# Linear attention of a hybrid layer taken four blocks at a time, with a new table of delays

## The chip, the cores and the metric

The kernel runs on one core of a Trainium2 chip. The metric is the device time of one execution in microseconds (us), as the median of three runs. Smaller is better. All arithmetic is float32; where the kernel uses the replicated form of it, `fp32r`, a float32 number is split into a high and a low part, and three products (high by high, low by high, high by low) take the place of one.

## The reference

One layer of a hybrid decoder with 1024 positions and 1024 channels. The normalised input goes through one wide projection, whose columns feed three groups: gated linear attention (GLA, 4 heads, key width 64, value width 128), an S5 state-space group with a Gelu and a gate, and an RG-LRU recurrent group. Their outputs go through one output projection, and a gated MLP with a short convolution follows. The part that the change touches is the GLA, which works on chunks of 64 positions:

```python
bc = jnp.cumsum(chunks(gk, DK), axis=3)              # log decay within a chunk
scores = einsum('bhncd,bhnsd->bhncs', qc * exp(bc - b_mid), kc * exp(b_mid - bc))
scores = jnp.where(causal, scores, 0.0)
o_intra = einsum('bhncs,bhnsv->bhncv', scores, vc)
kv = einsum('bhnsd,bhnsv->bhndv', kc * exp(b_last - bc), vc)
def step(S, inp):                                    # over the chunks
    dec, kv_n = inp
    return dec[..., None] * S + kv_n, S
o_inter = einsum('bhncd,bhndv->bhncv', qc * exp(bc), S_prev)
o = rmsnorm(o_intra + o_inter, norm_g) * silu(g)
```

## The kernel before

*How the order of the work comes about.* The program is written out once, on the host, in a single order. A small planner decides it: each piece of side work is a generator (`gla_task`, `gla_out`, the S5 and RG-LRU tasks, the gate `s5_glu`, `t_pre`), and each of its yields puts it back in a heap with a due time. `run(filler)` takes the task whose due time has come by a model clock `clk`, and otherwise lets the filler write one more piece of the big matrix products. Only matrix products move `clk` on. How long a task rests behind its yield is in the table `DLY`, under the task's name and the number of the yield. `ORDER` lists the column tiles of the wide projection in the order in which the filler comes to them. Every engine then works strictly in the order that was written, so DLY and ORDER set what stands behind what on each engine, in the queue of SyncE (SP), which issues the DMAs, too.

*The GLA.* Its heads come in two pairs (`p` = 0, 1: tasks gla0 and gla1), the 1024 positions in two halves (`hf`) of four blocks of 128 positions, that is of two chunks. `gla_prep` makes the decayed queries and keys of a half on VectorE (DVE) and ScalarE (ACT). TensorE (PE) transposes the keys (`psk2`; ACT copies them to `km`). Then the half goes in two steps `j` of two blocks each. A step writes the scores (`psc`) and their corrections for the second chunk against the first, lets DVE copy the causal part to a tile (`scb`, the trace calls some of these `gkw`) by a predicated copy, writes the key-value products of its two blocks into one PSUM tile (`pkv`), and DVE makes the next states from it (`S`, for every block a new one). After a rest the step writes the outputs (`po`): scores by values, and queries by state. `gla_norm` squares them on ACT (`sqo`), makes one factor per row and head on DVE and GpSimd (POOL, a power of -0.5, `ssg`), and scales them on ACT (`og`). When the half is done, `gla_out` transposes the outputs on PE (`pog`) and DVE multiplies them by the gate (`ot`).

*What stands around it.* The filler writes the wide projection (`pj`; its value columns `pv` are 256 wide), later the output projection (`po<-whi`), the up projection (`pd`) and the down projection (`dX`, `dY`). The S5 group has its output products (`psY`), its Gelu on ACT (`yg`), a turn through DRAM (`scr_y`, loaded back as `y`), its gate (`psglu`, `tg`, `ys`) and some small products (`tw` is a DVE tile of it). The RG-LRU group has its gates (`psrg`, `tr`). `t_pre` loads pieces of `w_down` (`rr`) and subtracts them from each other for the last stage. PSUM is shared out in three pools: two tiles for the filler, two named sm (`psk2`, `pkv`, `psY`, `psglu`, `psrg`) and four named gm (`psc`, `po`, `pog`). In the trace nearly every matrix product has line 184, transposes line 188, and the operations of DVE and ACT line 173, since helpers write them; so the rows are told apart by their tiles.

## Time and profile before

| | |
|---|---|
| median of three runs | 1049.54 us (1049.50 to 1049.83) |
| profiled execution, whole | 1048.84 us |
| its span (first to last instruction) | 1047.1 us |
| PE busy | 1015.6 us, 97% |
| DVE busy | 796.5 us, 76% |
| ACT busy | 437.1 us, 42% |
| POOL busy | 38.1 us, 4% |
| mean granted clock of PE | 0.998 |
| DMA, mean over the span | 140 GB/s |

The profile is of one execution. An engine is busy while an instruction of it runs; what it waits for shows as idle time ahead of an instruction, with the engine and tile that released it. The granted clock is the share of PE's full speed that the chip allowed in a stretch. PE is the engine with the most busy time; the others have idle time in every stretch, which costs nothing where PE does not wait for them.

### The profile page before, as it was taken

What the parts mean: (1) busy time and instruction counts of PE and PEld (TensorE: products, weight loads), DVE (VectorE), ACT (ScalarE), POOL (GpSimd) and SP (SyncE); (2) the same over time, 40 slices, a digit from 0 to 9 for tenths busy, and PEclk for the clock granted to TensorE, in tenths of its full rate; (3) what the DMA queues carried; (4) which work ended last, traced back from release to release, by engine and by line L of the source; (5) the groups of instructions that cost most, each with busy time, mean ns of one, the idle gap of its engine ahead of it and who ended that gap; (6) DMA issues with size and microseconds to landing.
All of it is one profiled execution on the core that took longest, in us unless ns stands there. A gap on an engine that the chain in (4) does not pass through costs nothing.

```text
span 1047.1 us, 13254 instructions
## 1 busy us (share of the span) xinstructions
PE 1015.6 (97%) x5012; PEld 834.7 (80%) x5012; DVE 796.5 (76%) x1328; ACT 437.1 (42%) x662; POOL 38.1 (4%) x54
## 2 busy tenths in 40 slices
PE   5999989999999999999999999999999999999997
PEld 4779777886778888888888888888888888888885
DVE  5896845678957987998878878878788747849865
ACT  6524243446644327453433334333333444323461
POOL 1200000200101001000000000000000000000010
PEclk9999999999999999999999999999999999999999
DMA  8142125882385014032323123232230697867722
GB/s 253 42 139 62 61 89 194 288 275 101 121 279 157 27 53 149 20 102 80 101 81 101 61 82 99 61 113 69 81 101 21 223 375 279 311 237 257 266 103 99
DMA packets 122933, 146.92 MB, mean 140 GB/s; under 512 B 9282, under 2 KB 79349, under 8 KB 122869
## 3 DMA queue, kind: packets, MB, share of 16 engines
q1 hardware_dynamic: 122868, 146.08, 42.0%
q8 instruction: 39, 0.64, 0.3%
q14 instruction: 26, 0.21, 0.1%
HBM read 111.45 MB, written 34.60 MB: 139 GB/s over the span
## 4 chain that ended last, share of the span: by engine, by line
PE 81%; DVE 3%; ACT 1%; DMA 1%; POOL 1%; issue 1%; DVEq 0%; POOLq 0%; ACTq 0%
PE pd L184 40%; PE dX L184 11%; PE po L184 9%; PE dY L184 9%; PE pj L184 7%; PE pv L184 2%; PE psglu L184 1%; DMA rr<-in_w_down_dram 1%; POOL ssg L1114 1%; PE pT L188 1%; PE psrg L184 0%; PE pog L188 0%; PE psc L184 0%; PE psY L184 0%; DVE rr L173 0%
## 5 line engine op out<-in xcount | busy, mean ns | idle before, releaser
L173 ACT CAST dhi<-rr 128x1024 fp32r<-128x1024 f32 (+1 forms) x78 | 72.5, 977 | 66.7 <-DVE rr L173 33.7
L173 DVE TENSOR_TENSOR dlo<-rr,dhi 128x1024 fp32r<-128x1024 f32 (+1 forms) x78 | 85.7, 1131 | 9.4 <-ACT dhi L173 8.9
L184 PE MATMUL pj<-hhi,whi 128*128 128x512 f32 x224 | 92.0, 411 | 0.0
L184 PE MATMUL pj<-hlo,whi 128*128 128x512 f32 x224 | 88.3, 394 | 0.7 <-DVE hlo L173 0.7
L184 PE MATMUL pj<-hhi,wlo 128*128 128x512 f32 x224 | 88.0, 393 | 0.0
L173 DVE TENSOR_TENSOR u<-u,pd 128x512 f32<-128x512 f32 x110 | 73.0, 683 | 9.8 <-PE pd L184 9.8
L173 DVE TENSOR_TENSOR xb<-u,pd 128x512 f32<-128x512 f32 x44 | 30.1, 685 | 63.6 <-PE pd L184 63.6
L173 ACT ACTIVATE ac<-xb,pc 128x512 f32<-128x512 f32 x44 | 35.6, 816 | 102.7 <-DVE xb L173 102.7
L184 PE MATMUL pd<-h2hi,hu 128*128 128x512 f32 x176 | 69.0, 392 | 0.0
L184 PE MATMUL pd<-h2hi,lu 128*128 128x512 f32 x176 | 68.5, 389 | 0.0
L184 PE MATMUL pd<-h2lo,hu 128*128 128x512 f32 x176 | 68.5, 389 | 0.0
L184 PE MATMUL pd<-h2hi,hA 128*128 128x512 f32 x176 | 68.5, 389 | 0.0
L184 PE MATMUL dX<-dhi,dlo 128*128 128x512 f32 x176 | 68.5, 389 | 0.0
L184 PE MATMUL pd<-h2hi,lA 128*128 128x512 f32 x176 | 68.5, 389 | 0.0
L184 PE MATMUL dX<-dlo,dhi 128*128 128x512 f32 x176 | 68.5, 389 | 0.0
L184 PE MATMUL pd<-h2lo,hA 128*128 128x512 f32 x176 | 68.5, 389 | 0.0
L184 PE MATMUL pd<-h2hi,hB 128*128 128x512 f32 x176 | 68.5, 389 | 0.0
L184 PE MATMUL pd<-h2lo,hB 128*128 128x512 f32 x176 | 68.5, 389 | 0.0
L184 PE MATMUL pd<-h2hi,lB 128*128 128x512 f32 x176 | 68.5, 389 | 0.0
L184 PE MATMUL dX<-dhi 128*128 128x512 f32 x176 | 68.5, 389 | 0.0
L173 DVE SCALAR_TENSOR_TENSOR ac<-xb,pc,ac 128x512 f32<-128x512 f32 x88 | 65.2, 748 | 2.2 <-ACT ac L173 1.6
L184 PE MATMUL pd<-h2hi,w 128*128 128x512 f32 x176 | 57.6, 389 | 0.0
(304 smaller groups left out, 2430.3 us busy)
## 6 DMA issues: line engine op xcount, KB each, us to landing
rr<-scr_a SPq DMA_DIRECT2D x45, 512.0 KB
rr<-in_w_down_dram SPq DMA_DIRECT2D x35, 512.0 KB
wu<-in_w_up_dram SPq DMA_DIRECT2D x22, 512.0 KB
wg<-in_w_up_dram SPq DMA_DIRECT2D x22, 512.0 KB
scr_a<-ac SPq DMA_DIRECT2D x22, 512.0 KB
scr_t<-rr SPq DMA_DIRECT2D x20, 512.0 KB
rr<-scr_t SPq DMA_DIRECT2D x20, 512.0 KB
raw<-in_w_in_dram SPq DMA_DIRECT2D x18, 512.0 KB
```

Of the source, the lines that this page charges most:

```text
L173: return fn(*a, **k)
L184: nc.tensor.matmul(ps, lhsT, rhs, start=start, stop=stop)
L188: nc.tensor.transpose(ps, src, ident if idn is None else idn)
L1114: G.tensor_tensor(ssg, ssg, mhalf[:, 0:4], op=ALU.pow)
```

## The change

A half of the GLA is no longer taken in two steps. `gla_task` writes the scores of all four blocks into two full PSUM tiles, then all corrections, then the key-value products of all four blocks (three in the second half, whose last state isn't needed) into one PSUM tile as one accumulation, then one predicated copy of 512 columns for each head, and then the state updates. After the rest all output products follow, and `gla_norm` is called once for eight columns in place of twice for four. A half has thus one rest ahead of its outputs and one behind them where it had two of each, and the keys of DLY for gla0 and gla1 go from 21 to 9 each. There is one set of two masked score tiles in place of two, and five state tiles in place of four. All other entries of DLY were drawn anew, and ORDER changes in its second half. Of the table two lines stand here.

```diff
-ORDER = [('s', 0), ('s', 1), ('q', 0), ('k', 0), ('gk', 0), ('v', 0), ('g', 0), ('g', 1), ('v', 1), ('q', 1), ('k', 1), ('rx', 0), ('rx', 1), ('g', 3), ('g', 2), ('rg', 0), ('rg', 1)]
+ORDER = [('s', 0), ('s', 1), ('q', 0), ('k', 0), ('gk', 0), ('v', 0), ('g', 0), ('g', 1), ('v', 1), ('q', 1), ('rx', 0), ('k', 1), ('g', 2), ('rx', 1), ('rg', 0), ('g', 3), ('rg', 1)]
...
-    ("gla0", 2): 8.72, ("gla0", 3): 2.05, ("gla0", 4): 0, ("gla0", 5): 0.74, ("gla0", 6): 0,
+    ("gla0", 2): 11.44, ("gla0", 3): 1.17, ("gla0", 4): 0, ("gla0", 5): 16.43, ("gla0", 6): 10.09,
...
@@ -965,15 +960,15 @@
         nc.sync.dma_start(wgk[16:32, :], gla_w_gk_up)
         mkf = GL["cv"]([P, P])
         cv3 = Carve("scb")
-        mk = cv3([P, 2, P], I32)
+        mk = cv3([P, 4, P], I32)
         V.memset(mkf, 1.0)
         G.affine_select(mkf, mkf, [[1, P]], ALU.is_ge, 0.0, base=0, channel_multiplier=-1)
-        for i in range(2):
+        for i in range(4):
             V.tensor_copy(mk[:, i, :], mkf)
-        scb = [cv3([P, 2, P]) for i in range(3)] + [GL["cv"]([P, 2, P])]
+        scb = [cv3([P, 4, P]), GL["cv"]([P, 4, P])]
         for s_ in scb:
             G.memset(s_, 0.0)
-        GL.update(wgk=wgk, mk=mk, scb=scb, isc=0)
+        GL.update(wgk=wgk, mk=mk, scb=scb)
 
     def gla_gate(p):
 
@@ -1050,70 +1045,63 @@
             A.copy(km, ps)
             og = st((P, 4, 2, P), f"og{p}{hf}")
             yield 1.0
-            for j in range(2):
-                psc = [gm("psc") for _ in range(2)]
-                for i in range(2):
-                    i4 = j * 2 + i
-                    for h2 in range(2):
-                        mm(psc[h2][:, i * P:(i + 1) * P], kt[halves[h2], i4 * P:(i4 + 1) * P], qb[halves[h2], i4], i == 0, i == 1)
-                for i in range(2):
-                    i4 = j * 2 + i
-                    for h2 in range(2):
-                        mm(psc[h2][0:64, i * P + 64:(i + 1) * P], kx[halves[h2], i4], hx[halves[h2], i4])
-                sc = []
+            vt = vts_[p, hf]
+            psc = [gm("psc") for _ in range(2)]
+            for i in range(4):
                 for h2 in range(2):
-                    sc.append(scb[GL["isc"] % NSC])
-                    GL["isc"] += 1
-                    V.copy_predicated(sc[h2], mk, psc[h2][:, 0:256].rearrange("p (i c) -> p i c", i=2))
-                S_in = []
-                for i in range(2):
-                    i4 = j * 2 + i
-                    b8 = hf * 4 + i4
-                    vt = vts_[p, hf][:, i4, :]
-                    S_in.append(S_prev)
-                    if b8 < 7:
-                        if i == 0:
-                            pkv = sm("pkv")
-                        for h2 in range(2):
-                            mm(pkv[halves[h2], i * P:(i + 1) * P], km[:, i4 * P + h2 * 64:i4 * P + (h2 + 1) * 64],
-                               vt[:, h2 * P:(h2 + 1) * P])
-                        S_new = ct([P, P], "S", bufs=4)
-                        if S_prev is None:
-                            V.tensor_copy(S_new, pkv[:, i * P:(i + 1) * P])
-                        else:
-                            V.scalar_tensor_tensor(S_new, S_prev, dblk[:, i4:i4 + 1], pkv[:, i * P:(i + 1) * P], MUL, ADD)
-                        S_prev = S_new
-                yield GLAD
-
-                po = [gm("po") for _ in range(2)]
-                for i in range(2):
-                    i4 = j * 2 + i
-                    vt = vts_[p, hf][:, i4, :]
-                    for h2 in range(2):
-                        mm(po[h2][:, i * P:(i + 1) * P], sc[h2][:, i, :], vt[:, h2 * P:(h2 + 1) * P], i == 0,
-                           i == 1 and S_in[1] is None)
-                for i in range(2):
-                    if S_in[i] is None:
-                        continue
-                    for h2 in range(2):
-                        mm(po[h2][:, i * P:(i + 1) * P], hb[halves[h2], j * 2 + i], S_in[i][halves[h2]], False, i == 1)
-                gla_norm(po, og[:, j * 2:j * 2 + 2])
-                if hf == 0 and j == 1:
-                    nxt = gla_prep(p, 1)
-                yield GLAD2
+                    mm(psc[h2][:, i * P:(i + 1) * P], kt[halves[h2], i * P:(i + 1) * P], qb[halves[h2], i], i == 0, i == 3)
+            for i in range(4):
+                for h2 in range(2):
+                    mm(psc[h2][0:64, i * P + 64:(i + 1) * P], kx[halves[h2], i], hx[halves[h2], i])
+            nkv = 4 - hf
+            pkv = sm("pkv")
+            for i in range(nkv):
+                for h2 in range(2):
+                    mm(pkv[halves[h2], i * P:(i + 1) * P], km[:, i * P + h2 * 64:i * P + (h2 + 1) * 64],
+                       vt[:, i, h2 * P:(h2 + 1) * P], i == 0, i == nkv - 1)
+            for h2 in range(2):
+                V.copy_predicated(scb[h2], mk, psc[h2].rearrange("p (i c) -> p i c", i=4))
+            S_in = [S_prev]
+            for i in range(nkv):
+                S_new = ct([P, P], "S", bufs=5)
+                if S_prev is None:
+                    V.tensor_copy(S_new, pkv[:, i * P:(i + 1) * P])
+                else:
+                    V.scalar_tensor_tensor(S_new, S_prev, dblk[:, i:i + 1], pkv[:, i * P:(i + 1) * P], MUL, ADD)
+                S_prev = S_new
+                S_in.append(S_new)
+            yield GLAD
+
+            po = [gm("po") for _ in range(2)]
+            for i in range(4):
+                for h2 in range(2):
+                    mm(po[h2][:, i * P:(i + 1) * P], scb[h2][:, i, :], vt[:, i, h2 * P:(h2 + 1) * P], i == 0, False)
+            for i in range(4):
+                if S_in[i] is None:
+                    continue
+                for h2 in range(2):
+                    mm(po[h2][:, i * P:(i + 1) * P], hb[halves[h2], i], S_in[i][halves[h2]], False, i == 3)
+            gla_norm(po, og)
+            if hf == 0:
+                nxt = gla_prep(p, 1)
+            yield GLAD2
             spawn(gla_out(p, hf, og), 3.0, f"go{p}{hf}")
         done.add(("gla", p))
 
-    def gla_norm(po, o2):
-
-        ssg = fxt([P, 4], "ssg", bufs=4)
-        junk = fxt([P, P], "sqo", bufs=2)
-        for j in range(4):
-            A.activation(junk, po[j // 2][:, j % 2 * P:(j % 2 + 1) * P], AF.Square, accum_out=ssg[:, j:j + 1])
+    def gla_norm(po, og):
+
+        ssg = fxt([P, 8], "ssg", bufs=2)
+        junk = fxt([P, P], "sqo")
+        for h2 in range(2):
+            for i in range(4):
+                j = h2 * 4 + i
+                A.activation(junk, po[h2][:, i * P:(i + 1) * P], AF.Square, accum_out=ssg[:, j:j + 1])
         V.tensor_scalar(ssg, ssg, 1.0 / P, EPS, MUL, ADD)
-        G.tensor_tensor(ssg, ssg, mhalf[:, 0:4], op=ALU.pow)
-        for j in range(4):
-            A.activation(o2[:, j % 2, j // 2, :], po[j // 2][:, j % 2 * P:(j % 2 + 1) * P], AF.Copy, scale=ssg[:, j:j + 1])
+        G.tensor_tensor(ssg, ssg, mhalf[:, 0:8], op=ALU.pow)
+        for h2 in range(2):
+            for i in range(4):
+                j = h2 * 4 + i
+                A.activation(og[:, i, h2, :], po[h2][:, i * P:(i + 1) * P], AF.Copy, scale=ssg[:, j:j + 1])
 
     def gla_out(p, hf, og):
```

What this does to the order is read from the instruction lists of both programs. The line numbers differ, since the new code is five lines shorter above (184 is 179 there, and 173 is 168). First PE, at the first half of the first head pair: the scores `psc`, the key-value products `pkv`, the outputs `po`, projections `pj` and `pv`, and the S5 products `psY` around them. Before:

```order
L184 MATMUL psc<-qh,ks 128x128 x4
L184 MATMUL psc<-pb,pc 64x64 x4
L184 MATMUL pkv<-v_924,pc 64x128 x4
L184 MATMUL pj<-hhi_148,whi 128x512
...
L184 MATMUL po<-v_924,scb 128x128 x4
L184 MATMUL po<-S,qh 128x128 x2
L184 MATMUL psY<-U_609,Mt_1028 128x128 x8
...
L184 MATMUL psc<-qh,ks 128x128 x4
L184 MATMUL psc<-pb,pc 64x64 x4
L184 MATMUL pkv<-v_924,pc 64x128 x4
```

And with the change, at the same place:

```order
L179 MATMUL psY<-U_609,Mt_1028 128x128 x8
...
L179 MATMUL pj<-hhi_142,whi 128x512
...
L179 MATMUL psc<-qh,ks 128x128 x8
L179 MATMUL psc<-pb,pc 64x64 x8
L179 MATMUL pkv<-v_924,pc 64x128 x8
L179 MATMUL pj<-hhi_145,whi 128x512
...
L179 MATMUL po<-v_924,scb 128x128
L179 MATMUL po<-v_924,gkw 128x128
...
L179 MATMUL po<-S,qh 128x128 x6
```

The first half of the S5 products moved from between the two steps to nine projections ahead of the scores; between `pkv` and the outputs stand six projections, where there were six and twelve value projections.

The second place is ACT, between the first half's outputs and the tanh of the gate (`tg`): squares `sqo`, scaled outputs `og`, the exponentials of the second half (`pa`, `b_`), the Gelu `yg`, and table loads. Before:

```order
L173 ACTIVATE sqo,ssg<-po 128x128 x4
L173 ACTIVATE og_1396<-po,ssg 128x128 x4
L173 ACT_TABLE_LOAD
L173 ACTIVATE yg<-psY 128x4x128 x4
L173 ACT_TABLE_LOAD
L173 ACTIVATE pa<-pa 128x512
L173 ACTIVATE sqo,ssg<-po 128x128 x3
L173 ACTIVATE b__945<-b__945 128x512
L173 ACTIVATE sqo,ssg<-po 128x128
L173 ACTIVATE pa<-pa 128x512 x2
L173 COPY pc<-psk_1702 128x512
L173 ACTIVATE og_1396<-po,ssg 128x128 x4
```

With the change:

```order
L168 ACTIVATE sqo,ssg<-po 128x128 x8
L168 ACTIVATE sg<-pj 128x512
L168 ACTIVATE og_1412<-po,ssg 128x128 x8
L168 ACT_TABLE_LOAD
L168 ACTIVATE pa<-pa 128x512
L168 ACTIVATE b__945<-b__945 128x512
L168 ACTIVATE pa<-pa 128x512 x2
L168 CAST whi<-raw 128x1024
L168 COPY v_1604<-pv 128x256
L168 ACT_TABLE_LOAD
L168 ACTIVATE yg<-psY 128x4x128 x2
```

The last two Gelus of four moved behind the whole norm of the first half and the exponentials of the second.

The third place is DVE, in the second half of the first head pair: masks, states `S`, gated outputs `ot`, the gate's result `ys`, and the subtractions `rr` of `t_pre`. Before:

```order
L173 TENSOR_TENSOR ot_1715<-pog,sg 128x512 x2
L173 TENSOR_TENSOR rr<-rr 128x512 x4
L173 SCALAR_TENSOR_TENSOR ys_1768<-tg,y_1605 128x8x128
L173 COPY_PREDICATED scb<-scb,psc 128x256 x2
L173 SCALAR_TENSOR_TENSOR S<-S,dblk,pkv 128x128 x2
L173 SCALAR_TENSOR_TENSOR ys_1849<-tg,y_1659 128x8x128
L173 TENSOR_TENSOR rr<-rr 128x1024
```

With the change:

```order
L168 TENSOR_TENSOR ot_1638<-pog,sg 128x512 x2
L168 TENSOR_TENSOR rr<-rr 128x512 x4
L168 SCALAR_TENSOR_TENSOR ys_1816<-tg,y_1464 128x8x128
L168 COPY_PREDICATED scb<-scb,psc 128x512
L168 COPY_PREDICATED gkw<-scb,psc 128x512
L168 SCALAR_TENSOR_TENSOR S<-S,dblk,pkv 128x128
L168 TENSOR_TENSOR rr<-rr 128x1024
L168 SCALAR_TENSOR_TENSOR S<-S,dblk,pkv 128x128
L168 TENSOR_TENSOR rr<-rr 128x1024
L168 SCALAR_TENSOR_TENSOR S<-S,dblk,pkv 128x128
L168 TENSOR_TENSOR rr<-rr 128x1024 x2
```

The three state updates of this half now have subtractions of 1024 columns between them.

## Rows read from the trace of the kernel before

**Rows 1.** The page's busy time of each engine, share of the span, instructions.

```profile
PE 1015.6 (97%) x5012; PEld 834.7 (80%) x5012; DVE 796.5 (76%) x1328; ACT 437.1 (42%) x662; POOL 38.1 (4%) x54
```

**Rows 2.** PE's waits: who waits, for what; us in all, times, the longest.

```profile
PE pkv L184 <- DVE S L173: 5.7, 6, 2.4
PE psrg L184 <- ACT tr L173: 1.6, 1, 1.6
PE pkv L184 <- ACT yg L173: 1.3, 1, 1.3
PE psk L188 <- DVE tw L173: 0.8, 1, 0.8
PE psk L188 <- DVE ssg L173: 0.8, 1, 0.8
```

**Rows 3.** PE in order of time: start, us, instruction, count, [idle before, releaser].

```profile
131.75 0.39 PE L184 MATMUL pj<-hlo,whi 128*128 128x512 f32 x1
131.98 0.39 PE L184 MATMUL pj<-hhi,wlo 128*128 128x512 f32 x1
132.30 0.71 PE L184 MATMUL psc<-qh,ks 64*128 64x128 f32 x8
133.32 0.44 PE L184 MATMUL pkv<-v,pc 128*64 128x128 f32 x4
...
136.17 0.44 PE L184 MATMUL pkv<-v,pc 128*64 128x128 f32 x4 [2.41 <-DVE S L173]
...
142.39 2.05 PE L184 MATMUL psY<-U,Mt 128*128 128x128 f32 x16
...
146.26 0.61 PE L184 MATMUL psc<-qh,ks 64*128 64x128 f32 x8
...
162.11 0.60 PE L188 MATMUL pog<-ident,og 128*128 128x128 f32 x4
```

**Rows 4.** Windows: us; busy PE, PEld, DVE, ACT, POOL; clock, DMA share, GB/s.

```profile
137.00:141.00 4.00, 4.00 (x19) 3.62 (x18) 2.39 (x4) 1.64 (x2) 0.00 (x0) 0.57 0.51 136
146.00:150.00 4.00, 2.30 (x34) 1.63 (x33) 1.24 (x4) 2.91 (x6) 0.00 (x0) 1.00 0.06 23
```

**Rows 5.** Timelines of ACT, SP's DMA queue and PE around the S5 group's gate.

```profile
153.83 1.09 ACT L173 ACTIVATE yg<-psY 128x512 f32<-128x512 f32 x2 [4.89 <-PE psY L184]
158.59 3.62 SPq L938 DMA_DIRECT2D y<-scr_y  x8
166.15 1.88 PE L184 MATMUL psglu<-y,smw 128*128 128x512 f32 x4
```

**Rows 6.** ACT's timeline at the first norm.

```profile
142.49 0.28 ACT L173 ACTIVATE sqo<-po 128x128 f32<-128x128 f32 x1 [3.08 <-PE po L184]
...
145.40 1.14 ACT L173 ACTIVATE og<-po,ssg 128x128 f32<-128x128 f32 x4 [1.34 <-POOL ssg L1114]
146.56 1.28 ACT L173 ACT_TABLE_LOAD   x1
```

**Rows 7.** POOL's timeline: two powers on four columns, one on eight.

```profile
144.35 1.02 POOL L1114 TENSOR_TENSOR ssg<-ssg,mhalf 128x4 f32<-128x4 f32 x1 [73.48 <-DVE ssg L173]
...
264.41 3.05 POOL L1114 TENSOR_TENSOR ssg<-ssg,mhalf 128x4 f32<-128x4 f32 x1 [9.89 <-DVE ssg L173]
...
334.53 1.64 POOL L836 TENSOR_TENSOR rs_r<-rs_r,mhalf 128x8 f32<-128x8 f32 x1 [14.24 <-DVE rs_r L173]
```

**Rows 8.** ACT's timeline at the exponentials of the second head pair.

```profile
228.37 0.63 ACT L173 ACTIVATE pa<-pa 128x512 f32<-128x512 f32 x1
...
231.63 1.04 ACT L173 CAST whi<-raw 128x1024 fp32r<-128x1024 f32 x1
```

**Rows 9.** DVE's timeline: masks, the first state, a subtraction for the last stage.

```profile
133.97 0.76 DVE L173 COPY_PREDICATED scb<-scb,psc 128x256 f32<-128x256 int32 x2
...
135.83 0.28 DVE L173 COPY S<-pkv 128x128 f32<-128x128 f32 x1
...
166.27 1.42 DVE L173 TENSOR_TENSOR rr<-rr 128x512 f32<-128x512 f32 x2 [2.83 <-DMA rr<-in_w_down_dram]
```

More of the change, by code (lines that the diff above doesn't have):

```diff
@@ L50 @@
 OPR = ("mg", "mggg", "mgsg", "ms")
-ORDER = [('s', 0), ('s', 1), ('q', 0), ('k', 0), ('gk', 0), ('v', 0), ('g', 0), ('g', 1), ('v', 1), ('q', 1), ('k', 1), ('rx', 0), ('rx', 1), ('g', 3), ('g', 2), ('rg', 0), ('rg', 1)]
+ORDER = [('s', 0), ('s', 1), ('q', 0), ('k', 0), ('gk', 0), ('v', 0), ('g', 0), ('g', 1), ('v', 1), ('q', 1), ('rx', 0), ('k', 1), ('g', 2), ('rx', 1), ('rg', 0), ('g', 3), ('rg', 1)]
 DLY = {
[9 rows of a table removed]
-    ("gla1", 20): 1.28, ("glu", 0): 0, ("glu", 1): 8.21, ("glu", 2): 1.5, ("glu", 3): 2.68,
[1 row of a table removed]
[4 rows of a table added]
+    ("gla1", 8): 4.14, ("glu", 0): 0, ("glu", 1): 9.45, ("glu", 2): 0, ("glu", 3): 1.21,
[1 row of a table added]
     ("gn003", 2): 2.2, ("gn011", 0): 5.67, ("gn013", 0): 11.25, ("gn013", 1): 0, ("gn013", 2): 1.7,
     ("gn101", 0): 2.54, ("gn103", 0): 5.32, ("gn103", 1): 2.28, ("gn103", 2): 1.6,
[3 rows of a table removed]
-    ("gsr", 0): 1.77, ("gsr", 1): 16.89, ("gss", 0): 0, ("gss", 1): 8.23, ("h2n0", 0): 3.35,
[7 rows of a table removed]
-    ("tab", 0): 3.78, ("tab", 1): 13.5, ("tab", 2): 10.69, ("tab", 3): 19.1, ("tpre", 0): 117.84,
-    ("tpre", 1): 9.22, ("tpre", 2): 9.1, ("tpre", 3): 0.14, ("tpre", 4): 8.8, ("tpre", 5): 6.35,
-    ("tpre", 6): 12.53, ("tpre", 7): 14.37, ("tpre", 8): 9.34, ("tpre", 9): 3.36,
-    ("tpre", 10): 18.52, ("tpre", 11): 0.13, ("tpre", 12): 8.99, ("xn1", 0): 2.39,
[3 rows of a table added]
+    ("gsr", 0): 1.34, ("gsr", 1): 36.39, ("gss", 0): 0, ("gss", 1): 30.61, ("h2n0", 0): 3.35,
[7 rows of a table added]
+    ("s51", 4): 3.87, ("tab", 0): 3.78, ("tab", 1): 13.93, ("tab", 2): 10.69, ("tab", 3): 19.59,
+    ("tpre", 0): 117.87, ("tpre", 1): 10.55, ("tpre", 2): 9.85, ("tpre", 3): 0, ("tpre", 4): 7.34,
+    ("tpre", 5): 8.22, ("tpre", 6): 15, ("tpre", 7): 9.7, ("tpre", 8): 7.96, ("tpre", 9): 0,
+    ("tpre", 10): 23.28, ("tpre", 11): 0, ("tpre", 12): 8.81, ("xn1", 0): 2.39,
 }
```

33 rows, old and new, of the table DLY are left out of this document.

## The prediction

> **What bounds the kernel now.** I read the page's busy times first: TensorE (PE) is busy for 1015.6 of 1047.1 us [rows 1], so a change is worth what it does to PE's work or to the 31 us in which PE waits. Then PE's waits by releaser [rows 2]: behind the start-up the largest is the key-value product (`pkv`) waiting for VectorE's state update (`S`), 5.7 us in six pieces, once 2.4. Then PE's order of time around the first pieces of the linear attention [rows 3], and the granted clock there [rows 4]. The reader is to see that two blocks' scores and products take about 1.4 us, that the second `pkv` stands still until VectorE has read the first one out of the same PSUM tile, and that right after the longest of these stops the clock is granted at 0.57 on the mean of 4 us, between the levels 2.4 and 1.2 GHz.
>
> **The change, part by part.** The profiled execution took 1048.84 us, 1.7 more than its span, and 0.7 less than the median of 1049.54. The sum is made against 1048.84, and 0.7 is put on at the end.
>
> *Work.* The matrix products are the same in number and shape: in order, eight score products and eight corrections stand in one run where two runs of four stood, eight `pkv` in place of two times four. So PE's own work does not shrink. What shrinks is the number of turns from the big projection products to small ones and back. Such a turn costs about 0.1 us on entering (0.32 from the last projection to the first score product against 0.23 between two projections [rows 3]) and I estimate the same on leaving. Between the first transposes of the attention and the output projection the new order has four such turns fewer, and one fewer later: 5 x 0.2, of which I count 0.6, since the transposes are cheaper turns. Bounds 0 and 1.0.
>
> *The wait that goes.* All `pkv` of a half stand before its first state update, so nothing on PE waits between them: six waits, 5.7 us, of which 2.41 is the longest, go [rows 2, 3]. In its place the state chain is late: it starts behind the fourth product instead of the first, and it is four updates long. What covers it is the work between `pkv` and the first use of a state, which is 6 projection products and the eight score-value products in the first half.
>
> *The wait for the Gelu.* 1.3 us of PE went to a `pkv` whose PSUM tile was still being read by the Gelu of the S5 group [rows 2]. The S5 output products now come 9 projections ahead of the first scores: 9 x 0.23 + 4 x 0.51 (a block's scores, 1.02 for two [rows 3]) = 4.1 us, against 1.09 for the two Gelus [rows 5]. It goes.
>
> *The clock.* 4 us at 0.57 lose 4 x 0.43 = 1.7 us of work [rows 4]. The 2.41 stop ends 0.8 us before them (136.17 [rows 3]); with the stop gone I count the 1.7 as gained. Bounds 0 and 1.7.
>
> *Three waits beside.* `psk<-tw` 0.8: VectorE's reading of the S5 tiles begins six projections (1.4 us) earlier in the order and has one more 0.6 instruction in it; 0.8 goes. `psk<-ssg` 0.8: the second half's transposes move behind 96 value projections (11 us), so its wait goes. `psrg<-tr` 1.6: ScalarE had the scaling of the attention output in front of that tanh, and in the new order has not; 1.6 goes. Together 3.2 [rows 2].
>
> *The norm.* It now comes once per half with eight columns in place of twice with four. ScalarE's squares cost 0.40 each (1.6 for four, from the first to the power's start at 144.35 less the 0.3 of VectorE [rows 6, 7]); eight take 3.2. The chain from the last output product to the first scaled column was 1.34 behind the squares, 1.01 of it GpSimd's power on four columns; on eight columns a power took 1.64 [rows 7]. So the first column is ready 3.2 + 1.96 = 5.2 us after the half's last product, the fourth at 6.3, the eighth at 7.5 (1.14 for four [rows 6]). PE reads the first four after 9 projections and 30 value projections: 9 x 0.23 + 30 x 0.115 (half the columns) = 5.5, and some turns. That is a wait of 0 to 1; I take 0.2. The same GpSimd power took 1.02 beside an idle VectorE and 3.05 beside a busy one [rows 7]. The Trainium skill (SBUF — State Buffer, Who interferes with whom) says that VectorE and GpSimd share one pair of ports, and that a VectorE instruction with two SBUF inputs blocks a GpSimd instruction that reads SBUF. By this rule the 0.2 would be up to 0.9 here, as one subtraction of 0.7 from SBUF [rows 9] stands beside the power; in the other three halves the readers come 3 us or more later, and the sum would be 0.7 higher, which the range holds.
>
> *A new lateness: the S5 group's gate.* Call A the end of the first half's output products. ScalarE now has, before the Gelu of the second S5 half: eight squares and the power (5.2), eight scalings (2.3), a table load (1.3 [rows 6]), the second half's exponentials with their waits for VectorE (3.3, from 228.37 to 231.63), a cast of 1.04 [rows 8], a copy of 0.35 and another table load of 1.3, and the Gelu of 1.1: it ends at A + 15.8. In the profile the gate's matmul `psglu` stood 11.2 us behind the end of that Gelu (154.92 to 166.15) without waiting, and the last of the eight loads that feed it was issued 7.3 us behind (162.21) [rows 5]. So its data come between A + 23.1 and A + 27.0. PE is there after 9 projections, 132 value projections, the S5 output products (3.9 from 142.39 to 146.26 [rows 3]) and twelve transposes of at most 0.15 [rows 3]: 2.1 + 15.2 + 3.9 + 1.5 and about 1 for turns = 23.7. Wait: 0 to 3.3; I take 1.2, a little under the middle.
>
> *The masks.* One masked copy of 512 columns replaces two of 256, which took 0.76 together [rows 9], so about 0.7 each. In the first half PE goes from the first score product to the first use of a mask in 2.0 + 4 x 0.4 + 6 x 0.23 = 5.0 us. If VectorE were free both masks and the first state would be there at 2.0 + 1.4 + 0.3 = 3.7. But three S5 instructions and a gate stand ahead of them in its queue; in before the masks started 0.7 us behind the start of the first `pkv` (133.32 to 133.97), and the first state 1.9 behind that [rows 3, 9]. I take 0.2; bounds 0 and 1.9.
>
> *The rest of the new table.* It moves the transposes of the second head pair to just behind the first recurrent group's VectorE work, and state updates between subtractions for the weights of the last stage. By the order these leave slacks of 0.5 to 3 us. Waits of this kind, which have nothing to do with `pkv`, were 3.3 us in before (0.8, 0.8, 1.6 [rows 2]); bounds 0 and 3.3 again, and I take 2.0.
>
> Sum: 5.7 + 1.3 + 1.7 + 3.2 + 0.6 = 12.5 gained; 0.2 + 1.2 + 0.2 + 2.0 = 3.6 lost; 8.9 net. 1048.84 - 8.9 = 1039.9, and with 0.7: **1040.6 us**.
>
> **Rivals.** *The gate becomes the new long stop.* If the S5 data come at the late end, PE stands 3.3 us before `psglu`, and a stop that long is followed by the low clock again: 2.1 more than counted plus 1.7, so 1040.6 + 3.8 = 1044.4. For it: the new table puts four weight loads ahead of the S5 store in SyncE's queue. Against it: these loads need only slots that PE has left by then. The Trainium skill (TensorE: Matmul & The Clock Gate, Why this matters for your kernels) holds that idle gaps between bursts lower the clock; here the stop of 2.41 was followed by the low clock, and the one of 1.3 for the Gelu was not (146 to 150 us at 1.00 [rows 4]). So a gate that waits as I forecast keeps the clock, and one that waits 3.3 does not.
>
> *Stop for stop.* In each of the four halves masks and states come later than PE needs them, since they now wait for four blocks: at the 1.9 of [rows 9] in each half, 7.6, less the 0.2 counted: 1048.0, no change. For it: VectorE is 76% busy and strictly in order. Against it: 21 projections (4.8 us) stand before the use in the third half, a gate product in the second, the output projection in the fourth.
>
> *Slower.* In the second half three state updates stand between subtractions of weights that come by DMA, and VectorE already waited 2.83 for such a load in before [rows 9]. If these loads land late, VectorE stops ahead of an update, PE stops at the output products of that half, and the low clock follows. Those products come 12 us behind the first `psglu`: four pairs of the gate's matmuls at 1.9 [rows 5], 12 value projections (1.4), the scores (2.0) and the products (1.1), and the loads are issued close behind the S5 loads. The forecast turns to slower by over 0.2% when this stop passes 8.9 + 2.1 = 11.0 us less 1.7 for the clock, so 9.3 us; at 10.5 it gives 1040.6 + 10.5 + 1.7 = 1052.8. Against it: they would have to land over 20 us behind the S5 loads, the last of which fed a matmul 3.9 us behind its issue (162.21 to 166.15 [rows 5]).
>
> That the change does not do what it says is shut out by the order: the eight `pkv` stand in a row, and the first of them alone has a wait.
>
> **How the numbers follow.** Forecast 0.70 (its own range 1037 to 1043.5), gate as long stop 0.14, stop for stop 0.08, slower 0.08. Below 1037 lies the case that the rest costs nothing (1040.6 - 3.6 = 1037.0) and the turns pay fully, so 1036.5 is the low end. The high end takes in the gate's case and part of the way to no change: 1046.5. Within 0.2% (2.1 us, about what a measurement here can tell from no change) falls the stop-for-stop case; faster 0.84, same 0.08, slower 0.08.
>
> **What would show it.** In the profile after: no row of `pkv` waiting for `S`; the granted clock at 1.00 from 100 to 400 us; a wait of `psglu` for its loads of about 1; `pog` waiting for `og` by under 1; no wait of `psrg` for `tr`; and PE's busy time unchanged or some us lower, as the low clock went. Wrong would be: `po` waiting for `scb` or `S` by over 1 us in several halves, `psglu` waiting 3 us or more with a clock below 1.00 behind it, or new waits in the up and down projections, whose order is nearly the same and which I count at nothing.

## The result, and the profile after

Four executions of the changed kernel took 1033.7 us in the median (1032.15 to 1034.5), the kernel before 1049.52 beside them: ratio 0.9849, with a 95% interval of 0.9837 to 0.9861. That is 15.8 us less where 9 were forecast, and 2.8 below the low end of the range. The direction was right; the size was not.

The page's busy line, and PE's waits, all that are there (who waits, for what: us in all, times, the longest), answer to [rows 1, 2]:

```profile
PE 1009.8 (98%) x5012; PEld 832.3 (81%) x5012; DVE 796.0 (77%) x1318; ACT 442.2 (43%) x666; POOL 33.0 (3%) x48
```

```profile
PE psR L183 <- DMA rows<-in_attn_norm_dram: 4.4, 1, 4.4
PE pT L183 <- DVE ss L168: 3.8, 2, 2.7
PE pT L183 <- DVE xt L168: 3.5, 2, 2.5
PE pj L179 <- ACT gl L168: 1.1, 1, 1.1
PE psR L183 <- DVE rows L168: 1.1, 1, 1.1
PE psC L183 <- ACT s5p L168: 0.6, 2, 0.5
PE pj L179 <- DVE hlo L168: 0.4, 1, 0.4
PE psW L183 <- ACT WTr L168: 0.2, 1, 0.2
PE pT L183 <- DVE h2lo L168: 0.2, 1, 0.2
```

Every wait of [rows 2] is gone, and one new one of 1.1 stands in the attention's part; the rest belongs to the start-up, and to the tables and the norm behind it. But PE's busy time fell too, by 5.8 us, with the same number of products. So not only waits went. The timeline of PE in the first half (start, us, instruction, count), beside [rows 3]:

```profile
134.04 1.16 PE L179 MATMUL psc<-qh,ks 64*128 64x128 f32 x16
135.13 0.68 PE L179 MATMUL psc<-pb,pc 64*64 64x64 f32 x16
135.74 1.09 PE L179 MATMUL pkv<-v,pc 128*64 128x128 f32 x16
...
140.40 0.94 PE L179 MATMUL po<-S,qh 64*128 64x128 f32 x12
```

Sixteen score products (the trace counts each of the attention's products twice) take 1.09 from their start to the next row's; eight took 0.64 before, from 132.30 [rows 3] to the row that follows there:

```profile
132.94 0.45 PE L184 MATMUL psc<-pb,pc 64*64 64x64 f32 x8
```

That is 0.055 for one and 0.20 for the run, and this fixed part is what the forecast did not see. I summed, for each kind of product, the times from one row's start to the next, less the idle time, from the attention's first transpose to the up projection (122.2 to 405.6 us before, 122.7 to 390.8 after). The wait of 0.8 for `tw`, just ahead of this stretch, stands with the waits, and three projections (0.7) that moved from the stretch to ahead of it are left out of its row:

| us | forecast | measured |
|---|---|---|
| PE's waits of before that go | -10.2 | -10.5 |
| new waits of PE | +3.6 | +1.1 |
| attention products beside the waits | -0.6 | -4.3 (`pkv` -2.0, `psc` and corrections -1.2, `po` -1.1) |
| all other work of this stretch (low clock, mostly) | -1.7 | -1.7 |
| ahead of and behind this stretch | 0 | +1.1 |
| sum, in the profiled executions | -8.9 | -14.3 |

The profiled execution of after (1034.50) was the slowest of its four, and that of before was 0.7 below its median; this makes 15.8 of the 14.3. The windows of the granted clock, beside [rows 4], show no dip (columns as there):

```profile
120.00:140.00 20.00, 19.92 (x176) 16.64 (x171) 19.69 (x38) 5.93 (x8) 0.00 (x0) 1.00 0.23 74
140.00:160.00 20.00, 19.94 (x175) 18.52 (x174) 10.67 (x19) 13.99 (x38) 1.65 (x1) 1.00 0.35 113
```

One correction to what stands ahead: the order that was written out holds for PE and SP. On DVE, ACT and POOL a scheduler with a timeline model (the kernel asks for it with `schedule_with_timeline_sim=True`, and exempts PE and SP with `manual_schedule`) orders the instructions anew, as the subtractions between three state updates of one step show in the order above. So moved code can move other DVE work too.

### The profile page after: what moved, and what is told of

The parts are those of the page before. It is cut to its first block, busy times and chain, and to the rows that moved or that the text cites. A ratio compares the mean times of both kernels' runs of the same rounds, so it can differ in the third digit from the quotient of the medians.

```text
span 1032.6 us, 13232 instructions
## 1 busy us (share of the span) xinstructions
PE 1009.8 (98%) x5012; PEld 832.3 (81%) x5012; DVE 796.0 (77%) x1318; ACT 442.2 (43%) x666; POOL 33.0 (3%) x48
## 4 chain that ended last, share of the span: by engine, by line
PE 92%; ACT 3%; DVE 2%; DMA 1%; POOL 1%; issue 0%; SPq 0%; DVEq 0%; POOLq 0%; ACTq 0%
PE pd L179 40%; PE pj L179 12%; PE dX L179 12%; PE po L179 10%; PE dY L179 9%; PE pv L179 4%; PE pT L183 1%; PE pgk L179 1%; PE psrg L179 1%; PE psglu L179 1%; PE psc L179 1%; DMA xt<-in_x_dram 1%; ACT sqo L168 1%; ACT junk L168 1%; DVE xc L168 0%
## 5 line engine op out<-in xcount | busy, mean ns | idle before, releaser
L168 ACT ACTIVATE ac<-ac 128x512 f32<-128x512 f32 x44 | 27.8, 633 | 75.1 <-DVE ac L168 75.1
```

The lines of the kernel that those rows point to most:

```text
L168: return fn(*a, **k)
```

## Experiments

Each group of kernels ran on a chip of its own, beside runs of the kernel before there. The runs of products, the unaltered kernel and the state update stand against 1049.45 in the median; the products together, code and table apart and the gate earlier against 1049.19; the lump parted against 1049.09; the preparation earlier against 1050.48; the filler between against a single 1048.10. "Slots" are the sums of the table above.

**Runs of products, cut in two and in four.** The same products, written by two blocks (below) or, with `range(0, 4, 1)`, by one:

```diff
-            for i in range(4):
-                for h2 in range(2):
-                    mm(psc[h2][:, i * P:(i + 1) * P], kt[halves[h2], i * P:(i + 1) * P], qb[halves[h2], i], i == 0, i == 3)
...
+            for j in range(0, 4, 2):
+                for i in range(j, j + 2):
+                    for h2 in range(2):
+                        mm(psc[h2][:, i * P:(i + 1) * P], kt[halves[h2], i * P:(i + 1) * P], qb[halves[h2], i], i == j, i == j + 1)
...
```

> The changed kernel, with the scores, corrections and key-value products of a half written in two runs of two blocks each, and the output products likewise; tasks, table, waits and every instruction are otherwise the same. Theory A (a run of small products has a fixed price, whatever stands beside it: from the changed kernel's PE rows 0.20 for the scores, 0.15 for the corrections, 0.15 for the key-value products, 0.1 and 0.2 for the two kinds of output products, 0.8 for a set): four sets more, +3.2 us on the changed kernel's 1033.7, so about 1036.9. Theory B (as the prediction counted it: only the turn from a projection to a small product and back costs): no such turn is added, 1033.7. In the profile A expects the slots of a half to grow by 0.8, B no growth.

> As the first, but in four runs of one block each. Theory A: twelve sets more, 12 x 0.8 = 9.6 less the key-value runs that the second halves don't have: about +9.3, so 1043. Theory B: 1033.7. A price that lies only in the first run of a kind would give the same as the two-run kernel.

> The changed kernel unaltered, for the spread and as the measure of the other three: 1033.7 within 1.2 (1032.2 to 1034.5 so far).

Measured: 1036.46 (1035.91 to 1037.79) and 1042.49 (1041.90 to 1043.53), with the unaltered kernel at 1033.97 (1033.58 to 1035.28): 2.5 and 8.5 more. In the slots of the five kinds it is 3.3 and 9.3, nearly as theory A has it, with waits as in the unaltered kernel; the start-up of the first happened to be 1.4 shorter. By the shapes that the rows print, the two kernels have 20 and 54 changes of tile shape more in this stretch than the unaltered one (48 and 82 against 28), so 0.165 and 0.17 for each. A piece of the four-run kernel (PE's timeline): four products take 0.42, 0.26 and 0.37 a kind, where 0.22, 0.11 and 0.22 are theirs by the long runs' slopes.

```profile
134.42 0.49 PE L179 MATMUL psc<-qh,ks 64*128 64x128 f32 x4
134.84 0.33 PE L179 MATMUL psc<-pb,pc 64*64 64x64 f32 x4
135.10 0.44 PE L179 MATMUL pkv<-v,pc 128*64 128x128 f32 x4
135.47 0.49 PE L179 MATMUL psc<-qh,ks 64*128 64x128 f32 x4
```

**Is it the kind of work, or the tile shape?** Filler pieces between the output products:

```diff
             for i in range(4):
+                if p == 0 and i:
+                    next(GL["body"], None)
                 for h2 in range(2):
                     mm(po[h2][:, i * P:(i + 1) * P], scb[h2][:, i, :], vt[:, i, h2 * P:(h2 + 1) * P], i == 0, False)
...
+                if p == 1 and i:
+                    next(GL["body"], None)
                 for h2 in range(2):
                     mm(po[h2][:, i * P:(i + 1) * P], hb[halves[h2], i], S_in[i][halves[h2]], False, i == 3)
...
+        body = GL["body"] = whole()
```

> The changed kernel with pieces of the filler (three projections each, that would have come behind) written between the output products: in the first head pair between the four blocks' score-value products (six pieces), in the second between the query-state products (five pieces between them, and one ahead). The first kind of product has the same tile shape in the profile as the projections (128*128), the second another (64*128). Theory A (the fixed price is paid where the tile shape changes, not where the kind of work does): the six pieces cost nothing, so the rows of the first pair show 0.22 to 0.24 for each pair of products whether a projection or a product stands behind them; the five cost 0.2 to 0.3 each, 1.0 to 1.5 in all, and a projection ahead of such products takes 0.32 in place of 0.23. Theory B (any turn between two kinds costs, as the prediction counted it, 0.2 there and back): 1.2 in the first pair and 1.0 in the second. One look; the time, 1034 to 1037, cannot tell these apart, the rows can.

A single execution. Pieces of the timeline, first pair, then second:

```profile
139.35 0.48 PE L179 MATMUL pj<-hhi,whi 128*128 128x512 f32 x1
...
140.13 0.38 PE L179 MATMUL po<-v,scb 128*128 128x128 f32 x2
140.35 0.39 PE L179 MATMUL po<-v,gkw 128*128 128x128 f32 x2
140.49 0.48 PE L179 MATMUL pj<-hhi,whi 128*128 128x512 f32 x1
...
257.06 0.49 PE L179 MATMUL po<-S,qh 64*128 64x128 f32 x4
257.48 0.50 PE L179 MATMUL pj<-hhi,whi 128*128 128x512 f32 x1
...
258.38 0.49 PE L179 MATMUL po<-S,qh 64*128 64x128 f32 x4
```

In the first pair a turn of three projections and four output products takes 1.14 (139.35 to 140.49): three at 0.23 and four at 0.11 make 1.13, so going there and back costs nothing. In the second it takes 1.32 (257.06 to 258.38), where 0.68 and 0.22 make 0.90: 0.42 for there and back, two changes, more than the 0.2 to 0.3 expected. In these rows the price hangs on the tile shape that they print, not on the kind of work. (The time, 1047.19, is that of new stops of 4.1, 3.3 and 1.2 us: the pieces came too early for ScalarE, and once for DVE.)

**The state update between the products**, in the changed kernel, with PE's order as it was:

```diff
-            for i in range(nkv):
-                for h2 in range(2):
-                    mm(pkv[halves[h2], i * P:(i + 1) * P], km[:, i * P + h2 * 64:i * P + (h2 + 1) * 64],
-                       vt[:, i, h2 * P:(h2 + 1) * P], i == 0, i == nkv - 1)
             for h2 in range(2):
                 V.copy_predicated(scb[h2], mk, psc[h2].rearrange("p (i c) -> p i c", i=4))
...
             for i in range(nkv):
+                for h2 in range(2):
+                    mm(pkv[halves[h2], i * P:(i + 1) * P], km[:, i * P + h2 * 64:i * P + (h2 + 1) * 64],
+                       vt[:, i, h2 * P:(h2 + 1) * P])
                 S_new = ct([P, P], "S", bufs=5)
```

> The changed kernel, with each state update written right behind its block's key-value products instead of behind all of them, and the masks ahead of these; PE's order is the same, word for word. Theory A (the waits for the state are what the old order paid): three stops in each first half and two in each second, 10 in all; the first of the first half about 2.8 (the state came 2.7 behind the first product in the changed kernel), the others 0.7 to 1.2: 9 to 10 us, and 1.0 to 1.5 for breaking the run of products in ten places, and up to 1.7 for a low clock behind the longest stop: 1044 to 1047. Rival (the stops are hidden, since PE would wait for the masks and states at the output products anyway): under 1037.

Measured 1061.97 (1061.32 to 1063.60), 28 more than the unaltered kernel: theory A in kind, more than twice its size. PE waited 17.9 us in ten stops, and 11.6 us went to the low clock and the broken runs. The longest stop, and the clock behind another (timeline, then windows):

```profile
308.20 0.44 PE L179 MATMUL pkv<-v,pc 128*64 128x128 f32 x4
315.76 0.69 PE L179 MATMUL pkv<-v,pc 128*64 128x128 f32 x4 [7.12 <-DVE S L168]
```

```profile
257.00:268.00 11.00, 9.18 (x32) 6.58 (x33) 3.50 (x7) 1.27 (x2) 0.00 (x0) 0.58 0.01 1
315.00:320.00 5.00, 3.79 (x16) 2.78 (x17) 2.69 (x6) 0.00 (x0) 0.00 (x0) 0.50 0.94 349
```

DVE came to the masks at 312.99, since it was at other work until then; the state stands behind them (DVE's timeline). I had taken the 0.7 of before for this, a size that did not hold here, where other work was queued ahead.

```profile
312.99 0.69 DVE L168 COPY_PREDICATED scb<-scb,psc 128x512 f32<-128x512 int32 x1
...
315.37 0.34 DVE L168 SCALAR_TENSOR_TENSOR S<-S,dblk,pkv 128x128 f32<-128x128 f32 x1
```

**The products together in the kernel before**, and nothing else:

```diff
+                for i in range(nkv):
+                    i4 = j * 2 + i
+                    vt = vts_[p, hf][:, i4, :]
+                    for h2 in range(2):
+                        mm(pkv[halves[h2], i * P:(i + 1) * P], km[:, i4 * P + h2 * 64:i4 * P + (h2 + 1) * 64],
...
                 for i in range(2):
...
-                            mm(pkv[halves[h2], i * P:(i + 1) * P], km[:, i4 * P + h2 * 64:i4 * P + (h2 + 1) * 64],
-                               vt[:, h2 * P:(h2 + 1) * P])
                         S_new = ct([P, P], "S", bufs=4)
```

> The kernel before, in which only this is changed: the key-value products of a step's two blocks stand behind each other and the two state updates behind both; steps, table and PE's order are as before. Theory A (the stops are what the old order paid, and work hides the later states): the six waits for the state go (5.7 us), seven breaks of the run of products go (7 x 0.15 = 1.0), and the low clock behind the longest stop goes (1.7): 8.4 less than 1049.5, so 1041.1; the wait for the Gelu (1.3) stays. Rival (stop for stop: the output products then wait for masks and states, up to 1.9 in each of the steps): 1047 to 1049.

Measured 1044.21 (1041.74 to 1044.42), 5.0 less than before, ratio 0.9946 (0.9929 to 0.9963): between the two. The six waits for `S` are gone and `pkv` takes 1.3 less beside them. Yet 3.2 came back as waits that the kernel before had smaller or not at all, and the low clock moved behind the first of them (PE's waits, then a window):

```profile
PE psrg L184 <- ACT tr L173: 3.0, 1, 3.0
PE pv L184 <- DVE sg L173: 1.8, 1, 1.8
```

```profile
263.00:268.00 5.00, 4.24 (x9) 2.50 (x10) 3.46 (x7) 4.36 (x7) 0.00 (x0) 0.70 0.88 294
```

**Code and table apart.** The new code with the old ORDER and DLY (but for gla0 and gla1), and the reverse:

> The changed kernel with the order of columns and all delays of the kernel before, but for the two attention tasks, which keep the new delays. Theory A (the new table took away the other four waits of before: Gelu 1.3, transposes 0.8 and 0.8, gates 1.6): these come back in part and new ones of the same size stand beside them, 3 to 8 us more than 1034.0, so 1037 to 1042. Rival (the table is neutral, and the four blocks alone took these waits away): 1033 to 1035.

> The kernel before with the new order of columns and all new delays, but for the two attention tasks, which keep their old code and delays. Theory A: the six waits for the state stay (5.7, as they lie inside a task's step), and the other four may go or be replaced: 1045 to 1050. Rival (the table alone gives most of the gain): under 1042.

Measured 1064.79 (1064.25 to 1067.39) and 1060.18 (1059.18 to 1062.37): 15.6 and 11.0 *slower* than the kernel before, far outside what either theory had. Neither half of the change alone is a gain. With the new table and the old code the six waits for `S` grow to 10.0 us, one of 3.5 for `og` and smaller ones stand beside them, and PE is busy 6.9 longer (1022.5), at a low clock behind the stops. With the old table and the new code PE waits twice for ScalarE to copy a filled PSUM tile, besides one wait of 3.0 for DVE (PE's waits):

```profile
PE pj L155 <- ACT xc L144: 9.9, 1, 9.9
PE pv L155 <- ACT v L144: 8.9, 1, 8.9
```

ScalarE's timeline shows why at the second of these: from 155.01 the eight squares, the wait for the power, eight scalings, a table load and the exponentials stand in one piece, and the copy of `v` behind them starts at 167.24.

```profile
160.51 2.17 ACT L144 ACTIVATE og<-po,ssg 128x128 f32<-128x128 f32 x8 [2.34 <-POOL ssg L1076]
162.70 1.28 ACT L144 ACT_TABLE_LOAD   x1
163.99 0.63 ACT L144 ACTIVATE pa<-pa 128x512 f32<-128x512 f32 x1
...
167.24 0.63 ACT L144 COPY v<-pv 128x256 f32<-128x256 f32 x2
```

**The lump parted.** To test that, the preparation of the second half (its exponentials) was put a rest behind the norm, with the old table and with the new. The table sets this rest to 6 and to 4 us, and makes the next one shorter by as much:

```diff
             gla_norm(po, og)
             if hf == 0:
+                yield 6.0
                 nxt = gla_prep(p, 1)
```

> The changed kernel with the old table (the sixth run: 1064.8, with PE once 8.9 us before a value projection and once 9.9 before a projection, since ScalarE had not copied the tile before), and in both heads the second half's preparation written 6 us of planner time behind the norm instead of with it, so that ScalarE can copy these tiles between the scaled outputs and the exponentials. Theory A (the lump on ScalarE, squares, power, scalings, table load, exponentials, some 13 us at a stretch, is what the old table lets PE run into): each of the two stops shrinks by the table load and the exponentials, 3 to 5 us, and the low clock behind them by a part: 1053 to 1060. Rival (the stops come from the places of the projections, whatever stands in the lump): 1062 or more.

> The changed kernel with its own table, and the same parting of norm and preparation with 4 us. Theory A: the one wait that the new order has left (1.1, a projection behind the Gelu of the recurrent group, which stands behind the exponentials on ScalarE) goes or shrinks, since the cast of the weights no longer stands between: 1032.6 to 1033.9. Rival (the second half's products come later and run into the state or the transposes): 1035 to 1038.

With the old table 1058.20 (1057.21 to 1058.86), 6.6 less; the stops shrank from 8.9 and 9.9 to 4.2 and 5.3, as theory A says. With the new table it was a miss: 1036.32 (1035.37 to 1036.91), in the range of the rival but not by its cause: the Gelu's wait grew to 2.4 (the exponentials now waited 1.91 for DVE at the new place) and one of 1.5 for `v` came.

**The gate earlier:** `("glu", 1): 9.45` became `5.45`.

> The changed kernel with the rest of the S5 gate's task shortened by 4 us in the table, so that PE comes to the gate's first product 4 us earlier, at about 161.3 in the time of the changed kernel's trace, where it came at 165.2 without waiting; the last load for it was issued at 163.7. Theory A (the data land within 1.5 us of the last issue, and the forecast's price of the gate was too high only since PE came just behind them): PE stops there for 2.5 to 4, a low clock follows for 0 to 4 us, and the time is 1036 to 1040. Rival (the loads land long before the last issue is through the queue, and there was never a lateness to be paid): no stop over 1, 1033 to 1035.

Measured 1044.34 (1042.87 to 1045.56), more than theory A had. PE stopped 3.8 for the loads, and the rest is the low clock and other waits, 3.2, of tasks that this moved (timelines of ACT and of PE, then a window):

```profile
155.69 1.09 ACT L168 ACTIVATE yg<-psY 128x512 f32<-128x512 f32 x2
```

```profile
160.00 1.02 PE L179 MATMUL psglu<-y,smw 128*128 128x512 f32 x2
164.87 5.46 PE L179 MATMUL psglu<-y,smw 128*128 128x512 f32 x6 [3.84 <-DMA y<-scr_y]
```

```profile
165.00:170.00 5.00, 5.00 (x7) 2.00 (x7) 0.00 (x0) 0.69 (x1) 0.00 (x0) 0.50 0.97 295
```

The data are there 8.1 behind the Gelu's end (156.78 to 164.87). So the gate's lateness is real, and the rival of this run is out. The first two products ran at once, at 160.00: they read the half of `y` that had been loaded earlier, and only the third reads the late one.

**The preparation earlier,** in the second head pair:

```diff
             yield GLAD
+            if hf == 0 and p == 1:
+                nxt = gla_prep(p, 1)
             po = [gm("po") for _ in range(2)]
...
-            if hf == 0:
+            if hf == 0 and not (hf == 0 and p == 1):
                 nxt = gla_prep(p, 1)
```

> The changed kernel with one thing moved: for the second head pair the preparation of the second half is written ahead of the first half's output products instead of behind their norm; PE's order is the same, word for word. In the changed kernel ScalarE is idle for 4.8 us ahead of the squares of that half and VectorE for 5.2 behind its states. Theory A (the wait of 1.1 behind the Gelu is the exponentials' place on ScalarE): the exponentials fall into that gap, the Gelu comes 3 us earlier, the wait goes, and nothing else waits: 1032.4 to 1033.4. Rival (VectorE now has the preparation between the state updates, and the output products wait for the states by as much or more): 1034 or more.

Measured 1032.69 (1031.76 to 1034.59), ratio to before 0.9834 (0.9821 to 0.9848), where the unaltered kernel had 0.9854 (0.9840 to 0.9869): about 1 us better in the median, but the intervals overlap, so the times don't show a gain. The profile is plainer: the last wait is gone, PE has none from the first transposes to the up projection, and that stretch takes 266.6 us where it took 268.0.

## Why the prediction was wrong

- *The waits that go* (5.7, 1.3 and 3.2): right; all are gone, 10.5 with the small one for `scb`. That it needs both halves of the change was not in the forecast. The products together alone gave 5.0 of the 8.4 expected, since PE then met DVE's and ScalarE's work elsewhere (3.2) and the low clock stayed; the changed kernel, with both halves, runs into neither.
- *Turns*: the step that failed most. "Such a turn costs about 0.1 us on entering ... 5 x 0.2, of which I count 0.6. Bounds 0 and 1.0." It counted only turns between projections and small products, and read the price of entering alone. The runs show a price at every change of tile shape, and a set of the attention's products has six of them where projections stand around it (64*128, 64*64, 128*64, back to 128*128, 64*128 and back). In the cut runs a set more brings five, since its kinds follow each other directly, and cost 0.82 (3.3 for four): about 0.165 a change. The changed kernel has 28 changes in the stretch where there were 48, and 20 at 0.165 make 3.3. The seven second runs of `pkv`, each begun anew behind a stop, make 1.0 at 0.15 each, and the products together alone took 1.3 off `pkv`; with the 3.3 that is 4.3 to 4.6, where 4.3 was measured against the 0.6 forecast. The upper bound of 1.0 had no row for leaving and none for the changes inside a set, and the low end of the range rested on it. In the trace before, eight corrections took 0.38 and sixteen take 0.61 now; a short and a long run of one kind side by side would have given the price (the kernel before had `po<-S` with both lengths: 0.42 for four, 0.65 for eight). The Trainium skill (TensorEngine Tiling (Array Packing), Key Properties) says that a change of tiling mode, unlike a change of tile, drains the engine. The filler between the products agrees: 0 at one shape, 0.42 there and back to another.
- *New waits* (3.6 with the gate, masks, norm and table): 1.1 was measured, so 2.5 too much. *The gate*: the chain was right to 0.1 (the Gelu ended at A + 15.7, forecast 15.8, with A at 141.26), and PE came at A + 23.9 (forecast 23.7). The data, by the 8.1 of the gate-earlier run, came at about A + 23.8 (an estimate), in the lower part of the 23.1 to 27.0, so there was no wait. The margin is larger than the forecast could see, since it counted from PE's first gate product, while the third is the first to need these data: about 0.9 later by the row below, so about 1.0 behind them. In the changed kernel:

```profile
146.51 2.18 ACT L168 ACTIVATE og<-po,ssg 128x128 f32<-128x128 f32 x8 [1.49 <-POOL ssg L1100]
...
155.86 1.09 ACT L168 ACTIVATE yg<-psY 128x512 f32<-128x512 f32 x2
```

```profile
165.20 3.60 PE L179 MATMUL psglu<-y,smw 128*128 128x512 f32 x8
```

The first of these two fences is ScalarE's timeline of the changed kernel at the norm and the second Gelu, the other PE's at the gate: no idle time stands in its row.

- *The norm*: the first scaled column came at A + 5.25 (forecast 5.2), and `pog` lost 0.4 in its own slot (0.76 where 0.35 is usual; forecast 0.2), as it had twice before the change (0.72). *The masks*: the first outputs lost some 0.2, as forecast.
- *POOL's power beside DVE*: in the first half it took 1.65 beside a subtraction of 0.69 that began 0.83 behind it, and 1.64 in the third and fourth, so the rule of the Trainium skill (SBUF — State Buffer, Who interferes with whom) did not show there. In the second half it took 3.33 beside a DVE instruction of 2.12 with two SBUF tiles that began 0.16 ahead of it, which agrees; nobody waited for it. POOL's timeline of the changed kernel:

```profile
144.83 1.65 POOL L1100 TENSOR_TENSOR ssg<-ssg,mhalf 128x8 f32<-128x8 f32 x1 [73.38 <-DVE ssg L168]
182.73 3.33 POOL L1100 TENSOR_TENSOR ssg<-ssg,mhalf 128x8 f32<-128x8 f32 x1 [36.26 <-DVE ssg L168]
```

- *The rest of the table* ("bounds 0 and 3.3"): one wait of 1.1 is left, for the Gelu `gl`, so the value of 2.0 was 0.9 too high. That the bounds held was luck: with other delays the same code ran into stops of 8.9 and 9.9. I took waits of before as an end for a quantity that hangs on a placing I did not check on ScalarE.
- *The clock*: right; no dip is left, 1.7. In the experiments the stops of 3.0, 3.8, 7.1 and 8.9 us each had a stretch of 0.50 to 0.70 behind them, that of 1.1 in the changed kernel none. The rule of the Trainium skill (TensorE: Matmul & The Clock Gate, Why this matters for your kernels) on idle gaps agrees with these. But the length of a stop alone does not decide it: behind one of 1.84 (old table, lump parted) the clock fell too, and behind one of 2.39 (new table, lump parted) it did not. Windows behind the stops of 8.9, 1.84 and 2.39, in this order, from three runs:

```profile
167.00:172.00 5.00, 4.36 (x21) 4.36 (x21) 2.83 (x5) 0.87 (x3) 0.00 (x0) 0.50 0.00 0
246.00:251.00 5.00, 4.75 (x8) 1.79 (x7) 0.47 (x2) 2.19 (x4) 0.00 (x0) 0.66 0.45 143
268.00:273.00 5.00, 4.81 (x21) 3.98 (x22) 4.35 (x5) 1.56 (x3) 0.00 (x0) 1.00 0.01 2
```

- *Rivals*: the gate as long stop, stop for stop and the slower case did not come; the first of them came in the gate-earlier run, so what kept it away was the placing. Stop for stop is partly what the products together alone gave. The three updates between subtractions were in time.

The sum in the profiled executions was 5.4 short: 3.7 from the turns and 2.8 from the waits, less 1.1 outside the stretch. What stays open is why a change costs more in the filler run (0.21) than in the cut runs (0.165), why the drawn table meets no long stop, and why the changed kernel's executions differ by 2.4 us.

## What to carry to other kernels

Look at the tile shape that the trace prints for each matrix product: products of one shape belong in long runs, and the price of a change is read from two runs of one kind with different lengths before any wait is counted. Taking one wait away can bring PE sooner to the next (3.2 of 5.7 came back with the products together): where an instruction order and its delays were drawn together, as here, neither half could be priced alone. Where one step puts a lump on an engine that also empties PSUM (here 12 us on ScalarE), ask first which matrix products need a free tile in that time.

## What the runs showed of the hardware

- A change of tile shape on TensorE cost about 0.17 us in the mean (3.3 for 20, 9.3 for 54), and 0.42 for a turn from 128*128 to 64*128 and back; a turn between different work at the same shape (128*128) cost nothing (1.14 for work of 1.13).
- Of the products with tile shape 64*128, which use the two halves of the rows in turn, one of 128 columns took 0.055 us in a long run, half of the 0.11 of those with 128*128.
- A stop of 7.1 us was followed by a granted clock of 0.50, the lower of the two levels, and so was one of 3.8; behind one of 1.84 it was 0.66 in the mean of 5 us, and behind one of 2.39 it stayed at 1.00.
